# Pacing three background tasks of a decoder block: the last gate, the second lot's operands and the final residual

## The chip, the cores and the metric

One core of one Trainium2 chip. The metric is the device time of one execution in microseconds, as the median of several runs.

## The reference

One decoder layer over 512 tokens of width 2048, in float32. A token mixer comes first (two attentions, gates, an output projection). Then the part that the change touches:

```python
x = x + (1 + gt1) * mixer(...)
h = rmsnorm(x, g_ffn) * (1 + sc2) + sh2
u = h @ w_up                                   # 2048 -> 2 * 5632
u = conv_b + sum(conv_w[i] * up[:, i:i + S] for i in range(3))   # causal, per channel
a, b = split(u, 2)
x = x + (1 + gt2) * ((silu(a) * b) @ w_down)   # 5632 -> 2048
out = rmsnorm(x, g_final)
# sh1, sc1, gt1, sh2, sc2, gt2 = split(silu(c) @ w_ada + b_ada, 6)
```

`gt2` is the "last gate": a product of the 2048 values of `silu(c)` with a 2048 x 2048 matrix.

## The kernel before

All large products run on TensorE (PE) in three passes: a weight tile is loaded (`load`, the `raw` buffers, eight of them, on the queue of SyncE, SP), rounded to a high part by ScalarE (ACT, L133, `wh`), and the rest is formed by VectorE (DVE, L135, `wl`). `mm3` (L143 to L145) then multiplies high by high, high by low and low by high. `F` is a set of 62 buffers of 128 x 512 that hold operands and results.

A tile framework orders the instructions of each engine by its own plan, from dependences, free buffers and the order in the program. Each engine then works in that order, and waits at an instruction until its data is there. `behind(pin)` adds one rule: what is written inside it stands after `pin` on `pin`'s engine.

Stages after the mixer: the output projection with the second norm at its end; a plain up-projection of the first three channel tiles (`plain`, L1095); then 41 units (`unit`, L207), each of which multiplies a pair of weight tiles with the normed tokens by Strassen-Winograd's scheme in seven products. A unit calls `between` twice, with its latest ACT and DVE instructions as pins. `finish` adds the convolution and the activation, and POOL stores the tile to `yd` in memory; the first three units also finish the three plain tiles.

The down-projection takes the 44 channel tiles in five lots: six plain, sixteen by Strassen (`strassen_down`, once for each half of the columns, with four groups and a call of `step` after each group of its two passes), two plain, sixteen by Strassen, and four plain. Partial sums go to memory (`sumd`) by accumulating DMAs of POOL (`add_to`). Each Strassen lot needs operand forms (`pair_forms`): sums, differences and splits of the tiles in `yd`, made before their group.

Three tasks run beside this:
- `last_gate` (L1167): 32 times, load half a row block of the gate's matrix into `soft` (one buffer), scale it by `silu(c)` on ACT, and accumulate it in memory; then sum over the partitions in four steps. `run(gate)` advances it by one step ahead of each unit.
- `forms2` (L1226): the forms of the second Strassen lot, whose tiles are loaded into the same `soft`.
- the end: for each of four token blocks and four column blocks, the last plain lot's four tiles are multiplied, `sumd` is added, the gate applied, and the residual `x1t` accumulated by a POOL DMA (in the last block it is loaded and added by DVE); squares are summed on ACT, and each token block is scaled and stored.

Of the kernel before, what the change touches and what calls it, by code (L numbers as in the profile page):

```python
# [36 lines left out]
NU = 3  # L37
# [39 lines left out]
def block_kernel(ctx: ExitStack, tc: tile.TileContext, A: dict, out: bass.AP):  # L77
# [7 lines left out]
    def nm(s):  # L85
        counter[0] += 1
        return f"{s}_{counter[0]}"
# [4 lines left out]
    def slot(dt=F32):  # L92

        return t2k("F", SLOTS, dt)
# [29 lines left out]
    def load(src, w=1024):  # L124
        raw = t2k("raw", 8, w=w)
        pins["load"] = nc.sync.dma_start(raw, src)
        return raw
# [2 lines left out]

    def parts(raw, w=1024):
        wh = t2k("wh", 3, F32R, w)
        act(wh, raw, AF.Copy)  # L133
        wl = t2k("wl", 3, F32R, w)
        tt(wl, raw, wh.bitcast(F32), ALU.subtract)  # L135
        return wh, wl

    def prep(src, w=1024):
# [21 lines left out]
    def split(src, hi=None, lo=None):  # L160
        hi = slot(F32R) if hi is None else hi
        pins["hi"] = act(hi, src, AF.Copy)
        lo = slot(F32R) if lo is None else lo
        tt(lo, src, hi.bitcast(F32), ALU.subtract)  # L164
        return hi, lo
# [6 lines left out]
    def form_t(f, b1, b2):  # L172

        t = t2k("sp", 2)
        tt(t[:, :HALF], b1[:, HALF:], b1[:, :HALF], ALU.subtract)
        tt(t[:, HALF:], b2[:, HALF:], t[:, :HALF], ALU.subtract)
        f["T1"], f["T2"] = halves(split(t))

    def form_u(f, b1, b2):
        t = t2k("sp", 2)  # L180
        tt(t[:, :HALF], b2[:, HALF:], b1[:, HALF:], ALU.subtract)
        tt(t[:, HALF:], b2[:, :HALF], b1[:, :HALF], ALU.subtract)
        tt(t[:, HALF:], t[:, HALF:], t[:, :HALF], ALU.subtract)
        f["T3"], f["T4"] = halves(split(t))
# [3 lines left out]
    def room(p):  # L188

        if p % 2 == 0:  # L190
            shared["B11"] = slot(F32R), slot(F32R)
        return tuple(x[:, p % 2 * HALF : (p % 2 + 1) * HALF] for x in shared["B11"])
# [549 lines left out]
    def run(work, n=1):  # L742
        for _ in range(n):
            last = next(work, None)
        return last
# [232 lines left out]
    def turn():  # L978

        if to_turn:  # L980
            j, x = to_turn.pop(0)
            ps = outs()
            for b in range(NQB):
                nc.tensor.transpose(ps[:, b * P : (b + 1) * P], x[:, b * P : (b + 1) * P], ident)
            o = slot()
            act(o, ps, AF.Copy)
            save(x1t[:, :, j * P : (j + 1) * P], o.rearrange("p (b f) -> p b f", b=NQB))
# [96 lines left out]
    def finish(j, ua, ub):  # L1084
        a = conv(ua, 2 * j)
        act(a, a, AF.Silu)
        b = conv(ub, 2 * j + 1)
        tt(a, a, b, ALU.mult)
        nc.gpsimd.dma_start(yd[j // 2][:, j % 2 * S : (j % 2 + 1) * S], a)
# [75 lines left out]
    gate_sum = [dr.tile([P, 1024], F32, tag=f"gates{half}", name=f"gates{half}") for half in range(2)]  # L1165

    def last_gate():  # L1167
        for k in range(KT):
            for half in range(2):
                w = sb.tile([P, 1024], F32, tag="soft", name=nm("soft"))  # L1170
                save(w, A["w_gate"][k, :, half * 1024 : (half + 1) * 1024])
                yield
                act(w, w, AF.Copy, scale=c_col[:, k : k + 1])  # L1173
                save(gate_sum[half], w, **({"accum_op": ALU.add} if k else {}))
        for b in range(4):
            w = sb.tile([P, 1024], F32, tag="soft", name=nm("soft"))
            save(w[:, :S], gate_sum[b // 2][:, b % 2 * S : (b % 2 + 1) * S])
            save(w[:1, S:], A["b_gate"][:, b * S : (b + 1) * S])
            yield
            ps = outs()  # L1180
            mm(ps[:1], ones[:, :1], w[:, :S], start=True, stop=True)
            stt(w[:1, S:], ps[:1], 1.0, w[:1, S:], ALU.add, ALU.add)
            save(gate_row[:, b * S : (b + 1) * S], w[:1, S:])

    gate = last_gate()
    for j in range(NU, NJ):
        run(gate)
        if j < 2 * NU:
            finish(j - NU, *ups[2 * (j - NU) : 2 * (j - NU) + 2])
        elif j < 2 * NU + 2:  # L1190
            x = t2k("T", 2)
            save(x, x1d[KT - 2 + j - 2 * NU])
            to_turn.append((KT - 2 + j - 2 * NU, x))
        finish(j, *unit(A["w_up"][j - NU], f, lambda *_: turn()))

# [12 lines left out]
    def plain_down(src, y, pairs, done):  # L1210

        n = 2 * len(pairs)
        for b in range(4):
            ps = bank(b)
            for c, p in enumerate(pairs):
                w = prep(src[b, c])
                if b == 0:
                    y.extend(two_tiles(p))
                for i in range(2):
                    k = 2 * c + i  # L1220
                    for t in range(NQB):
                        mm3(ps[t], cols(y[k], t), cols(w, i, S), k == 0, k == n - 1)
            for t in range(NQB):
                done((t, b), evac(ps[t]))

    def pair_forms(f, first, own=False):  # L1226
        for p in range(MID // 2):
            if own:
                r = sb.tile([P, 1024], F32, tag="soft", name=nm("soft"))
                nc.sync.dma_start(r, yd[first // 2 + p])  # L1230
            else:
                r = load(yd[first // 2 + p])
            b1, b2 = r[:, :S], r[:, S:]
            f[p]["B11"] = split(b1[:, :HALF], *room(p))
            form_t(f[p], b1, b2)
            form_u(f[p], b1, b2)
            f[p]["B21"], f[p]["B22"] = halves(split(b2))
            yield

    def strassen_down(v, src, f, done, step=lambda i: None):  # L1240
# [59 lines left out]
        add_to(sumd[tb], c)  # L1300

    f1, f2 = ([{} for _ in range(MID // 2)] for _ in range(2))
    forms1, forms2 = pair_forms(f1, AT[1]), pair_forms(f2, AT[3], True)
    made = [0]

    def first_sum(tb, c):
# [5 lines left out]
    plain_down(A["w_down0"], [], range(D0 // 2), first_sum)  # L1312
    run(forms1, MID)
    strassen_down(0, A["w_down1"][0], f1, keep)
    strassen_down(1, A["w_down1"][1], f1, keep, lambda i: run(forms2) if i in (2, 4, 6) else None)

    def second_sum(tb, c):
        keep(tb, c)
        if tb[0] == NQB - 1:
            run(forms2)  # L1320

    plain_down(A["w_down2"], [], range(AT[2] // 2, AT[3] // 2), second_sum)
    run(forms2, MID)


    base = {}

    def sum_here(tb, c):
        add_to(c, sumd[tb])
        base[tb] = c  # L1330

    strassen_down(0, A["w_down3"][0], f2, keep)
    y, last_w = [], {}

    def last_operands(i):
        if i == 3:
            for p in range(AT[4] // 2, NJ // 2):
                y.extend(two_tiles(p))
        elif i > 3:
            last_weights(i - 4)  # L1340
# [6 lines left out]

    strassen_down(1, A["w_down3"][1], f2, sum_here, last_operands)


    def row_of(src, b):
        r = slot()
        save(r, src[:, b * S : (b + 1) * S].to_broadcast([P, S]))
        return r

    row, g_row = ([row_of(src, b) for b in range(4)] for src in (gate_row, A["g_row"]))
    ps = []
    for t in range(NQB):
        xs = []
        s = sb.tile([P, NQB], F32, tag="s", bufs=2, name=nm("s"))  # L1360
        r = sb.tile([P, NQB], F32, tag="r", bufs=2, name=nm("r"))
        for b in range(2):
            base[t, b] = fetch(sumd[t, b])
        late = t == NQB - 1
        if late:
            before = [fetch(x1t[:, t, b * S : (b + 1) * S]) for b in range(4)]
        for b in range(4):
            if not ps:
                ps = bank(t)
            o = ps.pop(0)  # L1370
            for k in range(D2):
                mm3(o, cols(y[k], t), last_w[b, k], k == 0, k == D2 - 1)
            x = base[t, b]
            tt(x, o, x, ALU.add)
            tt(x, x, row[b], ALU.mult)
            if late:
                tt(x, x, before[b], ALU.add)
            else:
                add_to(x, x1t[:, t, b * S : (b + 1) * S])
            act(t2k("ta", 2), x, AF.Square, accum_out=s[:, b : b + 1])  # L1380
            if late and b < 2:
                tt(x, x, g_row[b], ALU.mult)
            xs.append(x)
        tt(r[:, :2], s[:, :2], s[:, 2:], ALU.add)
        tt(r[:, 2:3], r[:, :1], r[:, 1:2], ALU.add)
        act(r[:, 3:], r[:, 2:3], AF.Sqrt, scale=1.0 / D, bias=eps)
        nc.vector.reciprocal(r[:, 3:], r[:, 3:])
        for b, x in enumerate(xs):
            if late and b < 2:
                act(x, x, AF.Copy, scale=r[:, 3:])  # L1390
            else:
                stt(x, x, r[:, 3:], g_row[b], ALU.mult, ALU.mult)
            nc.sync.dma_start(out[t][:, b * S : (b + 1) * S], x)


def _layout(i):
# [101 lines left out]
```

## Time and profile before

| | us |
|---|---|
| median of 3 runs | 2950.79 (2948.07 to 2954.95) |
| the profiled execution | 2941.89 |
| its span, first to last instruction | 2940.1 |
| PE busy | 2804.4 (95%) |
| DVE busy | 2421.0 (82%) |
| ACT busy | 1465.1 (50%) |

Times in the profile count from the span's start. Lines such as L1173 are lines of the kernel before. In a group's line the last numbers are the idle time of the engine just before these instructions and what ended it; in a timeline that stands in brackets. An instruction's time includes its own latency, so that of two in a row on one engine the second can start before the first has ended.

### The profile page before, as it was taken

What the parts mean: (1) busy time and instruction counts of PE and PEld (TensorE: products, weight loads), DVE (VectorE), ACT (ScalarE), POOL (GpSimd) and SP (SyncE); (2) the same over time, 40 slices, a digit from 0 to 9 for tenths busy, and PEclk for the clock granted to TensorE, in tenths of its full rate; (3) what the DMA queues carried; (4) which work ended last, traced back from release to release, by engine and by line L of the source; (5) the groups of instructions that cost most, each with busy time, mean ns of one, the idle gap of its engine ahead of it and who ended that gap; (6) DMA issues with size and microseconds to landing.
All of it is one profiled execution on the core that took longest, in us unless ns stands there. A gap on an engine that the chain in (4) does not pass through costs nothing.

```text
span 2940.1 us, 47740 instructions
## 1 busy us (share of the span) xinstructions
PE 2804.4 (95%) x18780; PEld 2567.8 (87%) x18780; DVE 2421.0 (82%) x3452; ACT 1465.1 (50%) x2066; POOL 331.3 (11%) x549
## 2 busy tenths in 40 slices
PE   9999999999999999999988878999999999998996
PEld 7779999999997778899878878999999998886785
DVE  8979889888887998798666667889888897887784
ACT  5554444555547555344565444545545445545452
POOL 0000000100111211112311111000000000002103
PEclk9999999999999999999998889999999999999998
DMA  9954456555574658667766666333333336568657
GB/s 357 334 203 159 152 193 209 194 178 170 184 235 147 233 203 283 226 182 224 238 160 172 179 172 167 116 127 109 119 128 110 130 116 208 157 170 224 174 179 191
DMA packets 161637, 544.84 MB, mean 185 GB/s; under 512 B 21170, under 2 KB 21554, under 8 KB 161412
## 3 DMA queue, kind: packets, MB, share of 16 engines
q1 hardware_dynamic: 109156, 384.88, 39.6%
q0 software_dynamic: 51664, 156.52, 19.1%
q8 instruction: 147, 2.41, 0.3%
q14 instruction: 78, 0.64, 0.1%
q10 hardware_dynamic: 592, 0.39, 0.0%
HBM read 450.57 MB, written 87.73 MB: 183 GB/s over the span
## 4 chain that ended last, share of the span: by engine, by line
PE 70%; DMA 10%; issue 8%; DVE 8%; ACT 2%; POOL 2%; SPq 0%; POOLq 0%; DVEq 0%; ACTq 0%
PE att L145 11%; PE att L143 11%; PE att L144 11%; PE acc L143 11%; PE acc L145 11%; PE acc L144 11%; DMA gates<-soft 2%; DMA soft<-in_w_gate 2%; DVE wl L135 2%; DVE raw L290 2%; DVE F L164 1%; DMA raw<-in_w_va 1%; DMA soft<-yd 1%; DMA F<-x1t 1%; PE acc L709 1%
## 5 line engine op out<-in xcount | busy, mean ns | idle before, releaser
L133 ACT ACTIVATE wh<-raw 128x1024 fp32r<-128x1024 f32 (+2 forms) x795 | 832.2, 1051 | 992.1 <-PE acc L144 181.0
L135 DVE TENSOR_TENSOR wl<-raw,wh 128x1024 fp32r<-128x1024 f32 (+2 forms) x795 | 958.9, 1210 | 209.6 <-ACT wh L133 202.8
L143 PE MATMUL acc<-F,wh 128*128 128x256 f32 (+1 forms) x2504 | 733.2, 295 | 28.0 <-ACT wh L133 14.1
L145 PE MATMUL acc<-F,wl 128*128 128x256 f32 (+1 forms) x2504 | 735.9, 294 | 5.3 <-DVE wl L135 5.2
L143 PE MATMUL att<-F,wh 128*128 128x256 f32 (+1 forms) x2432 | 716.1, 297 | 23.5 <-ACT wh L133 19.3
L144 PE MATMUL acc<-F,wh 128*128 128x256 f32 (+1 forms) x2504 | 735.8, 294 | 0.0
L145 PE MATMUL att<-F,wl 128*128 128x256 f32 (+1 forms) x2432 | 718.4, 296 | 9.8 <-DVE wl L135 9.8
L144 PE MATMUL att<-F,wh 128*128 128x256 f32 (+1 forms) x2432 | 717.7, 295 | 1.2 <-DVE F L164 1.2
L143 PEld LDWEIGHTS acc<-F,wh 128*128 128x128 f32 x2504 | 483.5, 193 | 43.5 <-ACT wh L133 17.0
L143 PEld LDWEIGHTS att<-F,wh 128*128 128x128 f32 x2432 | 474.5, 195 | 37.3 <-ACT wh L133 22.0
L145 PEld LDWEIGHTS acc<-F,wl 128*128 128x128 f32 x2504 | 483.5, 193 | 16.4 <-DVE wl L135 7.5
L144 PEld LDWEIGHTS acc<-F,wh 128*128 128x128 f32 x2504 | 484.0, 193 | 9.9 <-DVE F L164 0.8
L145 PEld LDWEIGHTS att<-F,wl 128*128 128x128 f32 x2432 | 473.6, 195 | 20.5 <-DVE wl L135 13.1
L144 PEld LDWEIGHTS att<-F,wh 128*128 128x128 f32 x2432 | 474.6, 195 | 11.8 <-DVE F L164 4.3
L290 DVE SCALAR_TENSOR_TENSOR raw<-raw,raw 128x1024 f32<-128x1024 f32 x154 | 186.2, 1217 | 9.1 <-ACT raw L323 7.8
L143 PE MATMUL att<-wh,F 128*128 128x512 f32 x448 | 178.7, 400 | 10.4 <-ACT F L414 7.1
L144 PE MATMUL att<-wl,F 128*128 128x512 f32 x448 | 176.2, 393 | 5.0 <-DVE wl L135 5.0
L145 PE MATMUL att<-wh,F 128*128 128x512 f32 x448 | 175.6, 392 | 1.0 <-DVE F L164 1.0
L233 DVE TENSOR_TENSOR raw<-raw,raw 128x1024 f32<-128x1024 f32 x81 | 98.5, 1216 | 19.4 <-DMA raw<-in_w_x 14.8
L1173 ACT ACTIVATE soft<-soft,c_col 128x1024 f32<-128x1024 f32 x32 | 36.8, 1150 | 155.3 <-DMA soft<-in_w_gate 155.3
L144 PE MATMUL acc<-wl,F 128*128 128x512 f32 x288 | 112.4, 390 | 0.4 <-DVE wl L135 0.4
L145 PE MATMUL acc<-wh,F 128*128 128x512 f32 x288 | 112.2, 390 | 0.0
(350 smaller groups left out, 3730.2 us busy)
## 6 DMA issues: line engine op xcount, KB each, us to landing
raw<-in_w_up SPq DMA_DIRECT2D x164, 512.0 KB, 3.6
raw<-in_w_ada SPq DMA_DIRECT2D x154, 512.0 KB, 5.5
raw<-in_w_x SPq DMA_DIRECT2D x128, 512.0 KB, 4.3
raw<-in_w_down SPq DMA_DIRECT2D x104, 512.0 KB, 4.3
xd<-F POOLq DMA_DIRECT2D x64, 256.0 KB, 3.0
F<-xd POOLq DMA_DIRECT2D x64, 256.0 KB, 5.0
raw<-in_w_o SPq DMA_DIRECT2D x32, 512.0 KB, 4.5
soft<-in_w_gate POOLq DMA_DIRECT2D x32, 512.0 KB, 4.6
```

The source lines that it names most:

```text
L133: act(wh, raw, AF.Copy)
L135: tt(wl, raw, wh.bitcast(F32), ALU.subtract)
L143: mm(ps, ah, bh, start=first, stop=False, skip_group_check=not check)
L144: mm(ps, ah, bl, start=False, stop=False, skip_group_check=not check)
L145: return mm(ps, al, bh, start=False, stop=last, skip_group_check=not check)
L164: tt(lo, src, hi.bitcast(F32), ALU.subtract)
L233: last_v = tt(s, a21, a22, ALU.add)
L290: stt(raw, raw, 1.0, cb[half], ALU.mult, ALU.mult, accum_out=macc[:, t, half : half + 1])
L709: mm(dots[:, :W], both[:, b * P : (b + 1) * P], kiR[i][:, :W], start=i == 0, stop=i == 1)
L1173: act(w, w, AF.Copy, scale=c_col[:, k : k + 1])
```

## The change

Three things. The gate's loads go to SP; a step now ends after the load and again after the accumulate, and is called inside each unit, behind its pins. The second lot's tiles go by turns into `soft` and into the two `ta` buffers, each loaded one step before its use; their forms stand behind the splits of the group before. For the first two column blocks, gate and residual are applied to the partial sums beside the last Strassen half (`base_steps`) and written back; in the end only the last product times the gate is added there, and for the other two column blocks the residual is loaded a token block ahead. A token block's scaling and stores stand behind the second column block of the next.

```diff
     def parts(raw, w=1024):
-        act(wh, raw, AF.Copy)
+        pins["wh"] = act(wh, raw, AF.Copy)
-        tt(wl, raw, wh.bitcast(F32), ALU.subtract)
+        pins["wl"] = tt(wl, raw, wh.bitcast(F32), ALU.subtract)
...
     def last_gate():
         for k in range(KT):
             for half in range(2):
-                save(w, A["w_gate"][k, :, half * 1024 : (half + 1) * 1024])
+                nc.sync.dma_start(w, A["w_gate"][k, :, half * 1024 : (half + 1) * 1024])
                 yield
                 act(w, w, AF.Copy, scale=c_col[:, k : k + 1])
                 save(gate_sum[half], w, **({"accum_op": ALU.add} if k else {}))
+                yield
         for b in range(4):
             # both loads: save -> nc.sync.dma_start
...
             save(gate_row[:, b * S : (b + 1) * S], w[:1, S:])
+            yield
+
+    def beside_up(i, *pins):
+        turn()
+        with behind(*pins):
+            run(gate)
...
     for j in range(NU, NJ):
-        run(gate)
...
-        finish(j, *unit(A["w_up"][j - NU], f, lambda *_: turn()))
+        finish(j, *unit(A["w_up"][j - NU], f, beside_up))
...
-                if b == 0:
+                if len(y) < 2 * c + 2:
                     y.extend(two_tiles(p))
...
+    def pair_ahead(first, p):
+        src = yd[first // 2 + p]
+        if p % 2:
+            r = t2k("ta", 2), t2k("ta", 2)
+        else:
+            both = sb.tile([P, 1024], F32, tag="soft", name=nm("soft"))
+            r = both[:, :S], both[:, S:]
+        for i in range(2):
+            nc.sync.dma_start(r[i], src[:, i * S : (i + 1) * S])
+        return r
+
+    def forms_ahead(f, first):
+        n = MID // 2
+        r = [pair_ahead(first, p) for p in range(2)]
+        yield
+        for p in range(n):
+            if 1 <= p < n - 1:
+                r.append(pair_ahead(first, p + 1))
+            with behind(pins["wh"], pins["wl"]):
+                make_forms(f[p], p, *r[p])      # the body of pair_forms
+            yield
...
-    strassen_down(1, A["w_down1"][1], f1, keep, lambda i: run(forms2) if i in (2, 4, 6) else None)
+    y = []
+    def second_forms(i):
+        if i in (0, 1, 3, 5, 7):
+            run(forms2)
+        if i == 6:
+            y.extend(two_tiles(AT[2] // 2))
+    strassen_down(1, A["w_down1"][1], f1, keep, second_forms)
...
-        if tb[0] == NQB - 1:
+        if tb in ((NQB - 1, 1), (NQB - 1, 3)):
             run(forms2)
...
-    run(forms2, MID)
-    strassen_down(0, A["w_down3"][0], f2, keep)
+    strassen_down(0, A["w_down3"][0], f2, keep, lambda i: run(forms2) if i < 2 else None)
+    row0 = []                                   # two columns blocks of gate_row, in "ta"
+    def base_steps():
+        for n in range(10):
+            if n >= 2:
+                tb, x = at_work[n - 2]
+                save(sumd[tb], x)
+            if 1 <= n < 9:
+                (t, b), x = at_work[n - 1]
+                with behind(pins["wl"]):
+                    tt(x, x, row0[b], ALU.mult)
+                add_to(x, x1t[:, t, b * S : (b + 1) * S])
+            if n < 8:
+                tb = n % NQB, n // NQB
+                at_work.append((tb, fetch(sumd[tb])))
+            yield
...
     def last_operands(i):
+        run(bases)
...
-    row, g_row = ([row_of(src, b) for b in range(4)] for src in (gate_row, A["g_row"]))
+    row, g_row = rows_of(gate_row), rows_of(A["g_row"])   # two 128 x 1024 "raw" buffers each, over SP
...
+    x1_part = operands(0)                       # fetch sumd[t, 0:2] and x1t of column blocks 2 and 3
     for t in range(NQB):
+        ahead = operands(t + 1) if t + 1 < NQB else None
...
             x = base[t, b]
-            tt(x, o, x, ALU.add)
-            tt(x, x, row[b], ALU.mult)
-            # add_to(x, x1t[...]), or tt(x, x, before[b], ALU.add) in the last token block
-            act(t2k("ta", 2), x, AF.Square, accum_out=s[:, b : b + 1])
+            if b < 2:
+                part = t2k("w", 2)
+                tt(part, o, row[b], ALU.mult)
+                tt(x, x, part, ALU.add)
+            else:
+                tt(x, o, x, ALU.add)
+                tt(x, x, row[b], ALU.mult)
+                last = tt(x, x, x1_part[b - 2], ALU.add)
+            act(t2k("sp", 2), x, AF.Square, accum_out=s[:, b : b + 1])
...
+            if b == 1 and before:
+                finish_tokens(*before)          # reciprocal root, scaling and stores, as before
+        before = t, xs, s
+        x1_part = ahead
+    finish_tokens(*before)
```

More of the change, by code (lines that the diff above doesn't have):

```diff
@@ L1174, in last_gate @@
                 save(gate_sum[half], w, **({"accum_op": ALU.add} if k else {}))
+                yield
         for b in range(4):
             w = sb.tile([P, 1024], F32, tag="soft", name=nm("soft"))
-            save(w[:, :S], gate_sum[b // 2][:, b % 2 * S : (b % 2 + 1) * S])
-            save(w[:1, S:], A["b_gate"][:, b * S : (b + 1) * S])
+            nc.sync.dma_start(w[:, :S], gate_sum[b // 2][:, b % 2 * S : (b % 2 + 1) * S])
+            nc.sync.dma_start(w[:1, S:], A["b_gate"][:, b * S : (b + 1) * S])
             yield
@@ L1224, in plain_down, with pair_forms, make_forms @@
                 done((t, b), evac(ps[t]))
-    def pair_forms(f, first, own=False):
+    def pair_forms(f, first):
         for p in range(MID // 2):
[L1228 to L1237, printed above, removed]
+            r = load(yd[first // 2 + p])
+            make_forms(f[p], p, r[:, :S], r[:, S:])
+            yield
+    def make_forms(q, p, b1, b2):
+        q["B11"] = split(b1[:, :HALF], *room(p))
+        form_t(q, b1, b2)
+        form_u(q, b1, b2)
+        q["B21"], q["B22"] = halves(split(b2))
+    def pair_ahead(first, p):
[17 more added lines that the diff above has]
+                make_forms(f[p], p, *r[p])
             yield
@@ L1302, in block_kernel @@
     f1, f2 = ([{} for _ in range(MID // 2)] for _ in range(2))
-    forms1, forms2 = pair_forms(f1, AT[1]), pair_forms(f2, AT[3], True)
+    forms1, forms2 = pair_forms(f1, AT[1]), forms_ahead(f2, AT[3])
     made = [0]
@@ L1314, in block_kernel @@
     strassen_down(0, A["w_down1"][0], f1, keep)
-    strassen_down(1, A["w_down1"][1], f1, keep, lambda i: run(forms2) if i in (2, 4, 6) else None)
+    y = []
[5 more added lines that the diff above has]
+    strassen_down(1, A["w_down1"][1], f1, keep, second_forms)
     def second_sum(tb, c):
         keep(tb, c)
-        if tb[0] == NQB - 1:
+        if tb in ((NQB - 1, 1), (NQB - 1, 3)):
             run(forms2)
-    plain_down(A["w_down2"], [], range(AT[2] // 2, AT[3] // 2), second_sum)
-    run(forms2, MID)
+    plain_down(A["w_down2"], y, range(AT[2] // 2, AT[3] // 2), second_sum)
     base = {}
+    strassen_down(0, A["w_down3"][0], f2, keep, lambda i: run(forms2) if i < 2 else None)
+    y, last_w = [], {}
+    row0 = []
+    for b in range(2):
+        row0.append(t2k("ta", 2))
+        save(row0[b], gate_row[:, b * S : (b + 1) * S].to_broadcast([P, S]))
+    at_work = []
+    def base_steps():
[12 more added lines that the diff above has]
+            yield
     def sum_here(tb, c):
@@ L1330, in sum_here @@
         base[tb] = c
-    strassen_down(0, A["w_down3"][0], f2, keep)
-    y, last_w = [], {}
+    bases = base_steps()
     def last_operands(i):
+        run(bases)
         if i == 3:
@@ L1348, in block_kernel, with rows_of, operands, finish_tokens @@
     strassen_down(1, A["w_down3"][1], f2, sum_here, last_operands)
[L1351 to L1354, printed above, removed]
-    row, g_row = ([row_of(src, b) for b in range(4)] for src in (gate_row, A["g_row"]))
-    ps = []
+    run(bases, 10)
+    def rows_of(src):
+        both = [t2k("raw", 8, w=1024) for _ in range(2)]
+        for v, r in enumerate(both):
+            nc.sync.dma_start(r, src[:, v * 1024 : (v + 1) * 1024].to_broadcast([P, 1024]))
+        return [both[b // 2][:, b % 2 * S : (b % 2 + 1) * S] for b in range(4)]
+    row, g_row = rows_of(gate_row), rows_of(A["g_row"])
+    def operands(t):
+        for b in range(2):
+            base[t, b] = fetch(sumd[t, b])
+        return [fetch(x1t[:, t, b * S : (b + 1) * S]) for b in range(2, 4)]
+    def finish_tokens(t, xs, s):
+        r = sb.tile([P, NQB], F32, tag="r", bufs=2, name=nm("r"))
+        tt(r[:, :2], s[:, :2], s[:, 2:], ALU.add)
+        tt(r[:, 2:3], r[:, :1], r[:, 1:2], ALU.add)
+        act(r[:, 3:], r[:, 2:3], AF.Sqrt, scale=1.0 / D, bias=eps)
+        nc.vector.reciprocal(r[:, 3:], r[:, 3:])
+        for b, x in enumerate(xs):
+            if t == NQB - 1 and b < 2:
+                act(x, x, AF.Copy, scale=r[:, 3:])
+            else:
+                stt(x, x, r[:, 3:], g_row[b], ALU.mult, ALU.mult)
+            nc.sync.dma_start(out[t][:, b * S : (b + 1) * S], x)
+    ps, before = [], None
+    x1_part = operands(0)
     for t in range(NQB):
+        ahead = operands(t + 1) if t + 1 < NQB else None
         xs = []
         s = sb.tile([P, NQB], F32, tag="s", bufs=2, name=nm("s"))
[L1361 to L1366, printed above, removed]
         for b in range(4):
@@ L1373, in block_kernel @@
             x = base[t, b]
-            tt(x, o, x, ALU.add)
-            tt(x, x, row[b], ALU.mult)
-            if late:
-                tt(x, x, before[b], ALU.add)
-            else:
-                add_to(x, x1t[:, t, b * S : (b + 1) * S])
-            act(t2k("ta", 2), x, AF.Square, accum_out=s[:, b : b + 1])
-            if late and b < 2:
+            if b < 2:
+                part = t2k("w", 2)
+                tt(part, o, row[b], ALU.mult)
+                tt(x, x, part, ALU.add)
+            else:
+                tt(x, o, x, ALU.add)
+                tt(x, x, row[b], ALU.mult)
+                last = tt(x, x, x1_part[b - 2], ALU.add)
+            act(t2k("sp", 2), x, AF.Square, accum_out=s[:, b : b + 1])
+            if t == NQB - 1 and b < 2:
                 tt(x, x, g_row[b], ALU.mult)
             xs.append(x)
[L1384 to L1393, printed above, removed]
+            if b == 1 and before:
[3 more added lines that the diff above has]
+    finish_tokens(*before)
 def _layout(i):
```

## The prediction

> **What bounds the kernel now.** First the page: the share and clock of the engines in 40 slices, and the costliest groups.
>
> ```profile
> span 2940.1 us, 47740 instructions
> ...
> PE   9999999999999999999988878999999999998996
> ...
> PEclk9999999999999999999998889999999999999998
> ...
> L1173 ACT ACTIVATE soft<-soft,c_col 128x1024 f32<-128x1024 f32 x32 | 36.8, 1150 | 155.3 <-DMA soft<-in_w_gate 155.3
> ...
> raw<-in_w_up SPq DMA_DIRECT2D x164, 512.0 KB, 3.6
> ```
>
> TensorE is busy nearly throughout; what is to be won are its holes. They lie in three places: slices 20 to 24, slices 36 and 37, and the last. One ScalarE group sat idle 155.3 us, always for the same load. The busy times by stretch give the sizes (the second number is the length, then PE, PEld, DVE, ACT, POOL with counts, clock, DMA share, GB/s):
>
> ```profile
> 1424.00:1448.00 24.00, 19.68 (x139) 19.17 (x137) 10.59 (x17) 10.15 (x16) 9.83 (x18) 0.86 0.87 282
> 1448.00:1540.00 92.00, 76.04 (x461) 66.81 (x461) 61.07 (x127) 55.10 (x94) 13.69 (x22) 0.95 0.64 184
> 1540.00:1830.00 290.00, 241.33 (x1731) 233.45 (x1732) 191.66 (x227) 135.84 (x174) 42.40 (x63) 0.89 0.65 173
> 1830.00:2276.00 446.00, 446.00 (x3719) 446.00 (x3719) 397.17 (x466) 222.67 (x289) 11.91 (x22) 1.00 0.36 119
> 2596.00:2672.00 76.00, 76.00 (x337) 62.86 (x336) 61.05 (x71) 37.83 (x46) 5.74 (x7) 1.00 0.64 185
> 2672.00:2705.00 33.00, 23.08 (x101) 18.16 (x99) 22.05 (x34) 14.97 (x25) 10.47 (x12) 0.95 0.88 208
> 2705.00:2791.00 86.00, 79.55 (x335) 63.66 (x336) 66.59 (x80) 42.15 (x53) 11.29 (x13) 0.98 0.66 175
> 2791.00:2868.00 77.00, 76.58 (x338) 63.07 (x337) 63.28 (x69) 40.93 (x52) 7.56 (x10) 1.00 0.60 178
> 2868.00:2912.00 44.00, 43.97 (x194) 36.06 (x193) 23.23 (x41) 8.12 (x21) 20.62 (x31) 1.00 0.90 217
> 2912.00:2940.00 28.00, 0.00 (x0) 0.00 (x0) 13.17 (x26) 6.92 (x20) 2.87 (x4) 0.59 0.51 154
> ```
>
> From 1830 on, PE runs without a hole: 446.00 / 3719 = 0.1199 us a matmul of 256 columns, so 20.15 us a unit (7 products of 8 x 3). The 512-column ones take 76.00 / 337 = 0.2255 us. The same units before 1830 cost much more.
>
> **Why they do.** The gate's chain, from the timeline (POOL, then ACT):
>
> ```profile
> 1564.89 0.87 POOL L1174 DMA_DIRECT2D gates<-soft  x1 [7.82 <-ACT soft L1173]
> 1570.47 0.55 POOL L1171 DMA_DIRECT2D soft<-in_w_gate  x1 [4.72 <-DMA gates<-soft]
> 1575.89 0.86 POOL L1174 DMA_DIRECT2D gates<-soft  x1 [4.87 <-ACT soft L1173]
> 1434.03 1.15 ACT L1173 ACTIVATE soft<-soft,c_col 128x1024 f32<-128x1024 f32 x1 [6.09 <-DMA soft<-in_w_gate]
> 1455.88 1.15 ACT L1173 ACTIVATE soft<-soft,c_col 128x1024 f32<-128x1024 f32 x1 [1.79 <-DMA soft<-in_w_gate]
> 1537.28 1.15 ACT L1173 ACTIVATE soft<-soft,c_col 128x1024 f32<-128x1024 f32 x1 [4.75 <-DMA soft<-in_w_gate]
> 1574.44 1.15 ACT L1173 ACTIVATE soft<-soft,c_col 128x1024 f32<-128x1024 f32 x1 [6.41 <-DMA soft<-in_w_gate]
> ```
>
> One buffer: load, scale, accumulate to memory, load again, 11 us a round (1564.89 to 1575.89). Nothing paces it: it runs from before 1434 on as fast as it can, and each scaling stands at the head of ScalarE's queue while its data is under way. Behind it wait the splits that feed PE.
>
> **Term 1, the units (1540 to 1830).** At 0.1199 us the 1731 matmuls need 207.6 of 290 us; 82.4 are lost, 48.7 idle and the rest to the clock (0.89). With a pin behind the unit's own evacuation, and two turns a unit of load / scale and add, one gate step spreads over 20 us, the round of 11 us fits, and the load is issued nearly a unit before the scaling that needs it. What is late next: VectorE. It works 397.17 / 446 x 20.15 = 17.9 us a unit, and the first three units carry a second finish:
>
> ```profile
> L1080 DVE SCALAR_TENSOR_TENSOR w<-F,cw,w 128x511 f32<-128x511 f32 x44 | 32.7, 744 | 0.0
> L1088 DVE TENSOR_TENSOR w<-w,w 128x512 f32<-128x512 f32 x23 | 15.7, 682 | 0.0
> ```
>
> 4 x 0.744 + 0.682 = 3.7 us, so 21.6 against 20.15: 4.4 us over three units, and 3 for the start. Gain 75 (38, if the 32 scalings of 1.15 us came onto the path, to 82). The four summing steps keep their matmuls: no change. POOL sheds 32 issues of 0.55 us and never again waits for an accumulate to land; nobody waits for that.
>
> **Term 2, the plain up stage (1448 to 1540).** 9 tiles go in two halves (9 x 36 x 0.1199 = 38.8), 7 whole (7 x 18 x 0.2255 = 28.4): 67.2 of 92 us, 24.8 lost. Eight gate steps waited here (first and last quoted), all now behind unit 0. DVE (61.07) and ACT (55.10 less 8 x 1.15) stay under 67.2. The norm's second half, the last forms and the evacuation before unit 0 keep 9. Gain 16 (8 to 24.8).
>
> **Term 3, the end of the output projection.** The first step waited 6.09 us ahead of the norm's last pieces. Lost in 24 us: 4.3 idle and 0.14 x 24 = 3.4 of clock. The norm's chain has waits of its own: 4 (0 to 7.7).
>
> **Term 4, the second lot's forms.** The chain that ended last, then ACT's timeline:
>
> ```profile
> 2690.00 9.57 DMA soft<-yd
> ```
>
> ```profile
> 2699.59 0.42 ACT L162 ACTIVATE F<-soft 128x256 fp32r<-128x256 f32 x1 [11.04 <-DMA soft<-yd]
> ```
>
> Again one buffer, with ACT standing for the load; the evacuations behind it hold PSUM, and PE stands. From 2672 to 2791, 96 + 336 matmuls need 97.4 of 119 us: 21.6 lost. With two buffers each load is out a step (10 us or more) ahead of its use, over the 9.57 of the worst. The eight loads become sixteen of half the size; SP issues one in 0.33 us (row below) and idles otherwise: nothing. The price moves to 2596:2672, where up to two more pairs go (nine DVE operations each, of 512 columns or fewer, so at most the 0.68 us of such a row in term 6) and the two splits of the plain pair, now read ahead: 61 + 20 x 0.68 = 74.7 of 76 us, close under. I charge 2 there (0 to 5), and 5 for handovers that stay. Gain 14 (5 to 21).
>
> **Term 5, base steps beside the last unit pair (2791 to 2868).** Eight multiplies of 0.68 us make DVE 68.7 of 77. Eight fetches, accumulates and saves of 256 KB are 6.3 MB, 82 GB/s on top of 178; the stretches at 208 and 217 have a DMA share near 0.9, and the chain already passes through a weight load here:
>
> ```profile
> 2838.34 5.37 DMA raw<-in_w_down
> ```
>
> That load took 5.37 where 3.6 is usual for its size. Cost 3: three weight loads late by some 1 to 2 us each; 0 if the tiles are far enough ahead, 6 if a multiply also waits for its fetch with the splits behind it on DVE, or the steps' three buffers out of the 62 `F` are short. On POOL a save waits for its accumulate's landing, with only the next steps behind it. The wide rows now come over SP behind the last weights, in four issues where POOL had eight: nothing, while they land before the first block's sums.
>
> **Term 6, the tail.** PE's last matmul, ACT's wait, the last evacuation, the last stores:
>
> ```profile
> 2911.58 0.39 PE L145 MATMUL outs<-F,F 128*128 128x512 f32 x1
> 2919.94 0.63 ACT L1380 ACTIVATE ta<-F 128x512 f32<-128x512 f32 x1 [6.59 <-DMA F<-x1t]
> 2928.61 0.68 DVE L1374 TENSOR_TENSOR F<-outs,F 128x512 f32<-128x512 f32 x1
> 2934.38 1.95 SPq L1393 DMA_DIRECT2D out_x<-F  x4
> ```
>
> The span ends 28.1 us after PE, because the residual comes by accumulates that stand in a row. With it fetched ahead, DVE has ten operations a token block, and four more for the block before, whose end now stands behind the second column block: 14 x 0.68 = 9.5 of PE's 48 x 0.2255 = 10.8 us, so it keeps up. In this execution it took 2940.1 - 2928.6 = 11.5 us from the last evacuation to the end, with the same work in it; plus 1 of backlog, 12.5. Gain 15.6 (17 without backlog, 9 with a whole block's ending and evacuations, 14 x 0.68 less 2, in the way). The squares move to another buffer: nothing.
>
> **Sum.** 75 + 16 + 4 + 14 - 3 + 15.6 = 121.6 against the profiled execution's 2941.89: 2820.3. The median of the runs, 2950.79, is 8.9 higher; I forecast 2829 for it.
>
> **Rivals.**
> Down-projection gives it back: DVE at 74.7 of 76 and DMA near 0.9 cost what terms 4 and 6 bring; 2829 + 30 = 2859. For it: those shares. Against: the stretch from 1830 holds PE full with DVE at 89%.
>
> The scalings stay on the path, 32 x 1.15 = 37: 2866. For it: every wide split passes ACT. Against: ACT is at half (222.67 of 446).
>
> The change doesn't do all that it says, because the lost clock isn't from the holes: 0.11 x 290 = 32 stays, 2861. Two stretches:
>
> ```profile
> 1616.00:1618.00 2.00, 0.66 (x4) 0.48 (x4) 2.00 (x4) 1.95 (x3) 0.89 (x2) 1.00 0.79 260
> 1620.00:1623.00 3.00, 3.00 (x16) 3.00 (x16) 1.44 (x2) 1.05 (x1) 0.00 (x0) 0.50 0.87 311
> ```
>
> A hole under 2 us, then half clock; and none from 1830 to 2276, where there are no holes. So the clock follows even short holes, and comes back with them. [...]
>
> Slower: SP blocks the weights. The gate's loads now wait on SP for the accumulate before, and the up-projection's loads stand behind them.
>
> ```profile
> 1879.69 0.33 SPq L126 DMA_DIRECT2D raw<-in_w_up  x1
> 1896.02 1.21 DVE L233 TENSOR_TENSOR raw<-raw,raw 128x1024 f32<-128x1024 f32 x1
> 1898.47 0.37 ACT L269 ACTIVATE F<-att 128x256 f32<-128x256 f32 x1
> ```
>
> A tile loaded at 1879.69 (3.6 to land) is used at 1896.02: 12.7 us of lead. The scaling follows 1898.47, its accumulate lands some 7 us on (round above), at 1906; the next such loads are due 1896 to 1900. If the gate's load stood ahead of them they would come 10 us late, still inside the lead. Were the accumulate itself late, behind a store on POOL, the lead would be used up: from 16.3 us on, each of 36 units loses 3.6 and the kernel ends at 2829 + 130 = 2959. Against: in planned order the accumulate follows the scaling, so those loads should come first. [...]
>
> **Numbers.** Forecast 0.66 (own range 2808 to 2848), down-projection 0.13, scalings 0.10, clock 0.04, SP 0.03, others 0.04. The range 2804 to 2868 takes in the first four. Faster by over 0.2% (about what a measurement here can tell) 0.95, the same 0.02, slower 0.03.
>
> **What would show it.** Right: the scaling's idle (155.3) gone, PE full from unit 3 on at clock 1.0, its loads 20 us apart to about 2200; no ACT wait for yd; 12 to 13 us after the last matmul. Wrong: ACT or SP waits on soft in the units, PE holes before 2672 of today's scale, multiplies waiting for fetches in the last pair, rows late in the tail.

## The result

| | before | after |
|---|---|---|
| median of the runs, us | 2949.57 (4 runs, 2948.07 to 2954.95) | 2815.76 (4 runs, 2810.95 to 2819.28) |
| ratio after / before | | 0.9542 [0.9523, 0.9561] |
| profiled execution, us | 2941.89 | 2819.28 |
| PE / DVE / ACT busy | 95% / 82% / 50% | 98% / 86% / 52% |

The kernel became 134 us faster; the forecast was 2829, a gain of 122. Lines are those of the kernel after (the gate's load is L1172, its scaling L1174, its accumulate L1175), and in an experiment's fences those of its own kernel. First the page of the kernel after: PE and its clock in 40 slices, and the gate's loads.

```profile
span 2817.4 us, 47873 instructions
...
PE   9999999999999999999999999999999999999997
...
PEclk9999999999999999999999999999999999999998
...
soft<-in_w_gate SPq DMA_DIRECT2D x32, 512.0 KB, 3.8
```

Every slice but the last is full, at full clock: the two dents in the middle are gone, and the one at the end is smaller. The groups by line show the cause of the largest one gone as well, for the scaling that had 155.3 us of idle time before it:

```profile
L1174 ACT ACTIVATE soft<-soft,c_col 128x1024 f32<-128x1024 f32 x32 | 36.6, 1142 | 0.0
```

Busy times by stretch of the kernel after (columns as in the prediction): end of the output projection, plain up stage, first four units, the other units, last Strassen half, the last plain lot, the rest.

```profile
1433.00:1452.00 19.00, 17.17 (x141) 16.74 (x140) 11.40 (x20) 9.89 (x16) 8.85 (x16) 1.00 1.00 338
1452.00:1522.00 70.00, 69.24 (x460) 63.79 (x460) 62.24 (x128) 49.58 (x88) 2.67 (x5) 1.00 0.39 128
1526.00:1607.00 81.00, 80.23 (x664) 79.49 (x663) 74.05 (x91) 48.13 (x64) 7.59 (x12) 1.00 0.57 171
1607.00:2170.00 563.00, 563.00 (x4694) 563.00 (x4694) 500.67 (x587) 310.88 (x393) 40.40 (x57) 1.00 0.64 171
2674.00:2753.00 79.00, 77.31 (x337) 62.52 (x336) 65.76 (x73) 41.13 (x52) 16.93 (x24) 1.00 0.87 257
2753.00:2797.00 44.00, 44.00 (x196) 36.45 (x195) 29.03 (x51) 9.56 (x25) 17.17 (x27) 1.00 0.73 214
2797.00:2817.00 20.00, 0.52 (x3) 0.09 (x1) 12.46 (x25) 5.42 (x14) 0.00 (x0) 0.63 0.29 105
```

From 1607 on, behind the first four, the units run at 563.00 / 4694 = 0.1199 us a matmul. Two rows are worse than they need be: the last Strassen half takes 79 us where before's took 77, and 20 us follow the last matmul. Cut at the first and last matmul of each part, and set against the profiled execution of before, the terms came out so:

| term | forecast | measured | lengths, before and after |
|---|---|---|---|
| 1 units | -75 | -80.9 | 915.0, 834.1 |
| 2 plain up stage | -16 | -21.1 | 91.4, 70.3 |
| 3 end of the output projection | -4 | -5.8 | 30.0, 24.2 |
| 4 second lot's forms, down-projection up to the last half | -14 | -18.0 | 336.5, 318.5 |
| 5 last Strassen half | +3 | +2.3 | 76.9, 79.2 |
| 6 tail, last plain lot to the end | -15.6 | -8.2 | 71.8, 63.6 |
| sum | -121.6 | -131.7 | |

The first 1420 us, which the change does not touch, were 9.1 us longer in this execution of after than in that of before, so the two spans differ by 122.7 only. Over the 13 profiled executions of all kernels here the first matmul of the plain up stage came between 1446 and 1455 us, so that part varies by as much.

### The profile page after: what moved, and what is told of

It reads as the page before. It is cut to its first block, busy times and chain, and to the rows that moved or that the text cites. A ratio compares the mean times of both kernels' runs of the same rounds, so it can differ in the third digit from the quotient of the medians.

```text
span 2817.4 us, 47873 instructions
## 1 busy us (share of the span) xinstructions
PE 2763.3 (98%) x18780; PEld 2535.6 (90%) x18780; DVE 2427.0 (86%) x3464; ACT 1467.8 (52%) x2066; POOL 314.8 (11%) x519
## 4 chain that ended last, share of the span: by engine, by line
PE 73%; DVE 6%; DMA 4%; issue 3%; ACT 1%; POOL 0%; DVEq 0%; POOLq 0%; ACTq 0%; SPq 0%
PE att L145 12%; PE att L143 12%; PE att L144 12%; PE acc L145 10%; PE acc L143 10%; PE acc L144 10%; DVE wl L135 1%; DMA raw<-in_w_x 1%; PE acc L709 1%; PE acc L803 1%; PE outs L909 1%; DMA F<-sumd 1%; DMA F<-x1d 1%; PE acc L878 1%; DMA raw<-in_w_down 1%
## 5 line engine op out<-in xcount | busy, mean ns | idle before, releaser
L145 PE MATMUL att<-F,wl 128*128 128x256 f32 (+1 forms) x2432 | 710.2, 292 | 2.9 <-DVE wl L135 2.9
L144 PE MATMUL att<-F,wh 128*128 128x256 f32 (+1 forms) x2432 | 710.1, 292 | 1.2 <-DVE F L164 1.2
L143 PE MATMUL att<-F,wh 128*128 128x256 f32 (+1 forms) x2432 | 706.9, 293 | 2.9 <-DVE sp L273 1.6
L143 PEld LDWEIGHTS att<-F,wh 128*128 128x128 f32 x2432 | 466.3, 192 | 14.8 <-ACT wh L133 3.7
L144 PEld LDWEIGHTS att<-F,wh 128*128 128x128 f32 x2432 | 466.4, 192 | 11.9 <-DVE F L164 4.3
L145 PEld LDWEIGHTS att<-F,wl 128*128 128x128 f32 x2432 | 465.9, 192 | 12.0 <-DVE wl L135 4.6
L233 DVE TENSOR_TENSOR raw<-raw,raw 128x1024 f32<-128x1024 f32 x81 | 98.9, 1221 | 28.2 <-DMA raw<-in_w_x 21.1
L145 PE MATMUL acc<-wh,F 128*128 128x512 f32 x288 | 112.2, 389 | 0.0
L143 PE MATMUL acc<-wh,F 128*128 128x512 f32 x288 | 111.8, 390 | 0.0
```

Of the source, the lines that this page charges most:

```text
L143: mm(ps, ah, bh, start=first, stop=False, skip_group_check=not check)
L144: mm(ps, ah, bl, start=False, stop=False, skip_group_check=not check)
L145: return mm(ps, al, bh, start=False, stop=last, skip_group_check=not check)
L233: last_v = tt(s, a21, a22, ALU.add)
```

## The experiments

Theory: the gate's pace was the cost (a load-dependent scaling at the head of ACT's queue, unpaced), and POOL's queue is why the tail fell short. Each part was first run alone.

**The gate's part alone.** The kernel before with the new `last_gate`; forms and tail as before.

```diff
+    def beside_up(i, *pins):
+        turn()
+        with behind(*pins):
+            run(gate)
...
-        run(gate)
...
-        finish(j, *unit(A["w_up"][j - NU], f, lambda *_: turn()))
+        finish(j, *unit(A["w_up"][j - NU], f, beside_up))
```

> The kernel before with the gate's part of the change alone (loads on SP, two turns a step, called inside the units behind their pins). If the gate's scalings at the head of ScalarE's queue were the loss in all three stretches, this takes 5.8 + 21.1 + 80.9 = 108 us off, so about 2842 us, PE is full from the fourth unit on, and the clock stays at 1.0 there. If the other two parts of the change helped those stretches too, by freeing buffers or queues, it comes out above 2860.

2837.75 us, ratio 0.9615 [0.9596, 0.9634]: 115 of the 134 us. Its plain up stage is 70.3 us and its units 834.1, the same as in the kernel after to 0.1 us, and its down-projection keeps the holes of before. One stretch of its units, as long as the one of before that had PE at 241.33 and the clock at 0.89:

```profile
1520.00:1810.00 290.00, 289.24 (x2406) 288.50 (x2405) 260.58 (x309) 164.37 (x211) 23.09 (x34) 1.00 0.62 171
```

**Is it the queue or the pace?** Two kernels from this one. The first takes the pins away and keeps SP and the two turns a unit:

```diff
     def beside_up(i, *pins):
         turn()
-        with behind(*pins):
-            run(gate)
+        run(gate)
```

> As e1, but the steps are not held behind the unit's evacuation and sum: only the queue of the loads and their place in the program differ from before. Theory pace: nothing holds the chain back, so it again runs a round of some 10 us as fast as it can from the output projection's end on, ScalarE waits at the scaling in every round, and at least two thirds of the 108 us are lost again: 2910 to 2945 us. Rival queue: what cost the time was the load's place on POOL behind the accumulate; then this equals e1 within 6 us.

2915.97 us, ratio 0.988 [0.9861, 0.9899]. One of ACT's waits (us in total, times, longest), and the two stretches of the prediction, in the kernel without pins:

```profile
ACT soft L1174 <- DMA soft<-in_w_gate: 123.3, 30, 7.4
1448.00:1540.00 92.00, 79.62 (x488) 71.27 (x489) 66.67 (x133) 60.10 (x101) 10.82 (x16) 0.93 0.72 196
1540.00:1830.00 290.00, 254.02 (x1944) 246.69 (x1944) 211.15 (x250) 143.91 (x185) 29.76 (x40) 0.95 0.69 183
```

The scaling waits for its load 30 times again, and holes and clock loss are back. Without the pins the plan puts the steps ahead of their units: the loads are issued from 1430.75 on in rounds of 9 to 19 us instead of once a unit. Of the part's 115 us the pins carry 78 (2915.97 less 2837.75). The other 37 are the rest of the edit: two turns a step, the call inside the unit, and SP.

The second keeps the pins and puts the loads back on POOL (those of the summing steps too):

```diff
-                nc.sync.dma_start(w, A["w_gate"][k, :, half * 1024 : (half + 1) * 1024])
+                save(w, A["w_gate"][k, :, half * 1024 : (half + 1) * 1024])
```

> As e1, but the gate's loads stay on POOL's queue; the pins stay. Theory pace: a round of 11 us fits into a unit of 20 us on either queue, so this equals e1 within 6 us (0.2%). Rival queue: POOL stands for each accumulate to land, the loads come late and each of 32 steps costs 1 to 4 us: 2875 to 2950 us.

2837.08 us, ratio 0.9611 [0.9596, 0.9626]: the same as on SP. Its units are 834.1 us too. So with the pins the queue of these loads is worth nothing; what counts is where the step stands in the engines' order and how often it is called. How the 37 us divide was not tried: no kernel has the pins with one turn a unit.

**The second lot's forms alone.** The kernel before with `forms_ahead`, the two buffers and the steps behind each group.

```diff
-    forms1, forms2 = pair_forms(f1, AT[1]), pair_forms(f2, AT[3], True)
+    forms1, forms2 = pair_forms(f1, AT[1]), forms_ahead(f2, AT[3])
...
-    strassen_down(1, A["w_down1"][1], f1, keep, lambda i: run(forms2) if i in (2, 4, 6) else None)
+    strassen_down(1, A["w_down1"][1], f1, keep, second_forms)
...
-    strassen_down(0, A["w_down3"][0], f2, keep)
+    strassen_down(0, A["w_down3"][0], f2, keep, lambda i: run(forms2) if i < 2 else None)
```

> The kernel before with the second lot's part alone (two buffers by turns, loads a step ahead, forms behind the splits, plain tiles read ahead). If ScalarE standing for the tiles of the second lot was the loss between the second Strassen half and the last one, 17 to 18 us go: about 2932 us, with PE holes from 2672 to 2742 closed and at most 2 us of new ones before. If the weights or the accumulating DMAs were late by themselves, the holes stay and it is 2950 us within 6.

2937.96 us, ratio 0.9951 [0.9933, 0.9968]. From the second half of the first lot to the end of the first half of the second it takes 77.6 + 22.0 + 77.6 us, where before took 78.2 + 30.4 + 86.4: 17.8 less, and 14.6 by the medians. ACT's waits for these tiles from the middle of that stretch on, in the kernel before and then in this one:

```profile
ACT F L162 <- DMA soft<-yd: 23.2, 7, 11.0
```

```profile
ACT F L162 <- DMA soft<-yd: 2.0, 1, 2.0
```

Seven waits have become one.

**The end alone.** The kernel before with `base_steps` and the new tail.

```diff
     def last_operands(i):
+        run(bases)
...
-    row, g_row = ([row_of(src, b) for b in range(4)] for src in (gate_row, A["g_row"]))
+    row, g_row = rows_of(gate_row), rows_of(A["g_row"])
...
+    x1_part = operands(0)
     for t in range(NQB):
+        ahead = operands(t + 1) if t + 1 < NQB else None
```

> The kernel before with the end's part alone (base steps beside the last Strassen half, residual a block ahead, a block's ending one block later). By the two traces it should bring 8.2 us in the tail and cost 2.3 in the last Strassen half: 6 us net, 0.2%. By the forecast's term 6 it would bring 12 to 13 us net. The trace should show VectorE waiting some 8 us for the first fetch of a partial sum in the tail, as in the changed kernel.

2943.68 us, ratio 0.9972 [0.996, 0.9985], some 8 us less. The time after the last matmul is 17.6 us, not 12.5, and the last Strassen half 79.0. So the shortfall against the forecast's tail comes with this part alone, if smaller than in the kernel after. By the medians the three parts, each alone, bring 114.8, 14.6 and 8.3 us, 137.7 in sum, against 133.8 together.

**Why the tail is long.** In the kernel after, DVE's timeline at the start of the tail and at its end:

```profile
2757.70 0.68 DVE L1455 TENSOR_TENSOR w<-att,raw 128x512 f32<-128x512 f32 x1
2759.47 0.69 DVE L1455 TENSOR_TENSOR w<-att,raw 128x512 f32<-128x512 f32 x1 [1.09 <-PE att L145]
2762.19 0.69 DVE L1458 TENSOR_TENSOR F<-att,F 128x512 f32<-128x512 f32 x1 [2.03 <-PE att L145]
2770.73 0.69 DVE L1456 TENSOR_TENSOR F<-F,w 128x512 f32<-128x512 f32 x1 [7.84 <-DMA F<-sumd]
...
2806.05 0.68 DVE L1458 TENSOR_TENSOR F<-outs,F 128x512 f32<-128x512 f32 x1
```

L1455 multiplies a product by the gate, L1456 adds it to the partial sum, which comes 7.84 us after DVE is ready for it; L1458 adds a product of the other column blocks to its partial sum. POOL's timeline tells why:

```profile
2744.90 0.90 POOL L647 DMA_DIRECT2D F<-sumd  x1
2753.09 0.55 POOL L1377 DMA_DIRECT2D sumd<-F  x1 [7.28 <-DMA F<-x1t]
...
2755.64 5.52 POOL L1207 DMA_DIRECT2D F<-sumd  x6
2758.87 3.42 POOL L1377 DMA_DIRECT2D sumd<-F  x2
2763.76 1.07 POOL L647 DMA_DIRECT2D F<-sumd  x2 [1.48 <-DMA F<-sumd]
```

The first fetches of the tail (L647, 2763.76; the L647 of 2744.90 is still a base step's) stand in one queue behind a write-back that waits 7.28 us for the accumulate before it, behind the accumulates of the last half's sums, and behind two more write-backs. The theory is this queue. Rivals: the write-back and second fetch alone make the sums late; or buffers come late whatever the queue. First the write-backs were taken away: the bases stay in their `F` buffers.

```diff
-            if n >= 2:
-                tb, x = at_work[n - 2]
-                save(sumd[tb], x)
...
+                base[t, b] = x
...
-        for b in range(2):
-            base[t, b] = fetch(sumd[t, b])
```

> The changed kernel, but the eight gated sums of the base steps stay in their F buffers: not written back to memory, and not fetched again for the tail. Theory: the tail is 20 us and not 12.5 after the last matmul because VectorE waits 7.8 us for the first of these fetches, which stands on POOL behind the accumulates of the last Strassen half, and 9.5 of 10.8 us of work a block leaves no room to catch up. Then 7 to 8 us go (ratio to the changed kernel 0.9973, about 2808), with 12 to 13 us from the last matmul to the end. Rival: the residual's fetches or the accumulates behind them are as late; then 2 us or less go.

2810.18 us, ratio 0.9522 [0.9508, 0.9536]; 16.1 us after the last matmul, better than 20.0 and short of the forecast's 12.5. The write-backs were part of it only: the wait moved to the residual, whose fetch has the same place on POOL:

```profile
2766.98 0.69 DVE L1456 TENSOR_TENSOR F<-F,F 128x512 f32<-128x512 f32 x1 [5.37 <-DMA F<-x1t]
```

Then the base steps were left out, and all four column blocks got gate and residual in the tail, fetched a token block ahead:

```diff
     def last_operands(i):
-        run(bases)
...
-            if b < 2:
-                part = t2k("w", 2)
-                tt(part, o, row[b], ALU.mult)
-                tt(x, x, part, ALU.add)
...
+            tt(x, o, x, ALU.add)
+            tt(x, x, row[b], ALU.mult)
+            last = tt(x, x, x1_part[b], ALU.add)
```

> The changed kernel without the base steps: gate and residual of all four column blocks are applied in the tail, with sums and residual fetched a block ahead. VectorE then has 16 x 0.68 = 10.9 us a block against PE's 10.8. The last Strassen half should lose its 2.3 us of holes. If writing back and fetching again is what delays the tail, the fetches come early here, and the tail ends 14 to 18 us after PE (now 20): 4 to 8 us faster than the changed kernel. If the base steps are worth what they take off VectorE, the tail ends 22 us or more after PE, and it is no faster.

2807.94 us, ratio 0.9513 [0.95, 0.9527]. The last half is back at 76.6 us, and 15.0 follow the last matmul, again with a wait for a fetch on POOL:

```profile
2752.34 0.69 DVE L1446 TENSOR_TENSOR F<-att,F 128x512 f32<-128x512 f32 x1 [5.36 <-DMA F<-sumd]
```

The base steps spare DVE operations in the tail; without them the tail is no longer, and the last half gets 2.6 us back.

**The queue by itself.** In each of the three kernels the tail's fetches went to SP (`fetch_sp` is a fetch issued there), with the kernel after run beside them. The edit to the kernel after; those to the other two are alike:

```diff
     def operands(t):
         for b in range(2):
-            base[t, b] = fetch(sumd[t, b])
-        return [fetch(x1t[:, t, b * S : (b + 1) * S]) for b in range(2, 4)]
+            base[t, b] = fetch_sp(sumd[t, b])
+        return [fetch_sp(x1t[:, t, b * S : (b + 1) * S]) for b in range(2, 4)]
```

> The kernel after, with the tail's fetches (the partial sums of the first two column blocks and the residual of the other two) issued on SP instead of POOL; nothing else differs. Theory (POOL's in-order queue: the fetches stand behind the six accumulates that end the last Strassen half, each waiting for an evacuation): VectorE's waits of 1.78 and 7.84 us for the first partial sums go, the stretch after the last matmul falls from 20.0 to 13 to 15 us, the time by 4 to 7 us against the kernel after. Rival (the fetches are late because their buffers come free late or because the write-backs land late, on whatever queue): the waits stay, under 1.5 us gained.

> The kernel without base steps (all four column blocks get gate and residual in the tail), with the tail's fetches on SP. Theory (POOL's queue): the waits of 5.36 and 1.78 us for the first partial sum go, 15.0 after the last matmul becomes 12 to 13, about 10 us faster than the kernel after. Rival (VectorE is short of room in the tail itself, 4 x 3 + 2 operations and the ending of the block before for each of four blocks): 15 stays, as without SP, about 8 us faster than the kernel after.

> The kernel with the bases of the first two column blocks kept in their buffers, with the residual of the other two fetched on SP. Theory (POOL's queue): the wait of 5.37 us for the residual goes, 16.1 after the last matmul becomes 12 to 13, about 7 us faster than the kernel after. Rival (buffers of F late): 16 stays.

> The kernel after itself, unchanged, timed beside the three others on one chip, so that they can be compared with it directly: 2812 to 2820, 20 us after the last matmul.

| | median, us | ratio to before | last Strassen half | after the last matmul |
|---|---|---|---|---|
| after, again | 2816.54 (2812.23 to 2818.08) | 0.954 [0.9525, 0.9555] | 78.7 | 19.0 |
| after, fetches on SP | 2807.26 (2804.59 to 2809.74) | 0.9512 [0.9497, 0.9527] | 79.0 | 12.0 |
| bases kept, on SP | 2806.81 (2806.31 to 2809.15) | 0.9512 [0.9498, 0.9527] | 78.4 | 12.9 |
| no base steps, on SP | 2804.30 (2800.89 to 2805.40) | 0.95 [0.9486, 0.9515] | 76.9 | 12.6 |

One changed queue takes 9 us off the kernel after by the medians, a little more than the 4 to 7 expected. Of the 10.7 us between the two profiled executions 7.0 lie after the last matmul, where 12.0 are left; the rest lies ahead of the tail, 2.4 of it before the plain up stage, and is not shown to be the queue's. In the other two kernels the same move shortens that stretch by 3.2 us (16.1 to 12.9) and 2.4 (15.0 to 12.6). From the timelines of SP and DVE, and the last stretch, of that kernel:

```profile
2744.00 1.50 SPq L1424 DMA_DIRECT2D F<-sumd  x2
2752.82 0.68 DVE L1460 TENSOR_TENSOR w<-att,raw 128x512 f32<-128x512 f32 x1
2753.54 0.69 DVE L1461 TENSOR_TENSOR F<-F,w 128x512 f32<-128x512 f32 x1
2794.35 0.68 DVE L1463 TENSOR_TENSOR F<-outs,F 128x512 f32<-128x512 f32 x1
2793.00:2805.00 12.00, 0.46 (x3) 0.04 (x1) 5.78 (x12) 3.07 (x7) 0.00 (x0) 0.73 0.38 131
```

SP issues the first fetches at 2744.00, six microseconds before the last half ends (in the kernel after, POOL did so ten microseconds behind that end). The add (L1461) follows its product (L1460) at once: no wait of DVE for a fetch is longer than 1.0 us. SP too waits for write-backs to land there, 17.6 us in three waits, so it is not their landing by itself that held DVE. And the tail follows DVE's first wait for a sum: 5.8 us with the end alone, 6.9 in the second run of the kernel after and 7.84 in the first go with 17.6, 19.0 and 20.0 us after the last matmul.

In the tail the queue of the plain fetches counts, by 7.0 us, because on POOL they stood behind accumulates and write-backs of other blocks. The gate's loads stand behind an accumulate too, but one whose landing they need on either queue, since both use the one buffer: POOL waits for it 216.0 us in 31 waits, SP 229.5 in 30, and moving them was worth nothing. The rival that DVE lacks room in the tail is out for the kernel without base steps too: 12.6 against 15.0. That kernel is the fastest by the medians: it beats the kernel after by 12 us, without overlap of the runs. So the base steps, one of the three parts of the change, bring nothing once the fetches are early (2807.26 with them, 2804.30 without).

## Why the prediction was right, and where it was off

Terms 1 to 3 were right in mechanism. The signs asked for are there: the scaling's idle is gone, PE is full from the units' start but for 0.8 us, and from the second on the loads come 17 to 25 us apart. They were undersized by 5.9, 5.1 and 1.8 us, mostly since the deductions did not come in full: by their first matmuls the first five units took 20.59, 20.82, 21.47, 20.44 and 20.48 us, 3.0 us above 20.15 in sum where 7.4 was charged, and the plain stage keeps 3 of the 9 us of evacuation and last forms charged there. The loss itself was a little larger than read: of the 1731 matmuls 12 are small ones that turn tiles, and the first ten units of before, taken one by one, lost 84.0 us and not 82.4. The splits of the 41 units hide the scalings wholly: that rival (2866) is refuted by the 0.0 of idle time and by units at PE's own pace.

Term 4 was undersized by 4.0. The crowded half came as charged, or nearly: from its own first to its last matmul the second half of the first lot, where the work went, takes 77.8 us where it took 76.4, 1.4 of the 2 charged, and the hole behind it is gone (77.6 against 78.2 to the next part's first matmul). Of the 5 us for handovers 1.9 stayed: 22.0 + 77.3 against the 97.4 that the matmuls need. Down-projection as a place that gives the gain back is refuted, except for these 1.4 us and its last half.

Term 5 was right: +2.3 where +3 was forecast, and +1.5 to +2.1 in the other kernels with base steps. Late weight loads are there as it said: in the last half ACT waits four times for one ahead of a rounding, 5.2 us in sum, in the kernel without base steps, with the fetches on SP, once, 1.6. Without base steps the 2.3 are gone. The 5.37 us that it took for a slow load, against 3.6, is no outlier, though: the median of these loads in this half of before is 5.1. The kernel with the gate's loads on POOL, which has no base steps either, has 78.6 us there, so a part of this size can also come otherwise.

Term 6 is the step that failed: forecast 12.5 us after the last matmul, 20.0 measured. Of its two pieces one held. From the last evacuation to the end of the span it is 2817.4 - 2806.05 = 11.4 us, forecast 11.5. The other, the backlog, was put at 1 us and was 2806.05 - 2797.4 = 8.6. The prediction said of the residual "with it fetched ahead", and never put these fetches in POOL's order behind the accumulates of the last half and the write-backs of its own base steps. Of a base step's save it said that it waits "with only the next steps behind it"; the tail's fetches stood behind it as well. DVE, with 9.5 of 10.8 us a token block, could catch up only part of a late start: its first sum started 16.9 us after the tail's first matmul, against 3.8 with the fetches on SP. On SP the pieces are 2805.5 - 2794.35 = 11.2 and 0.9 us, which is the forecast's tail.

**The 8.9 us for the median.** This step was wrong too. The excess of the median over the profiled execution was carried over to the kernel after as if it lay in parts that stay. Two kernels that leave the units as they were, the one with the forms alone and the one with the end alone, show the same 290 us:

```profile
1540.00:1830.00 290.00, 234.56 (x1655) 226.35 (x1655) 183.31 (x218) 130.47 (x166) 42.41 (x63) 0.88 0.65 169
1547.00:1837.00 290.00, 237.58 (x1686) 229.47 (x1686) 185.82 (x220) 131.91 (x168) 42.45 (x63) 0.88 0.66 172
```

Against 1731 matmuls in the execution of before that is 76 and 45 fewer, at 0.1199 us 9.1 and 5.4 us. Their first part was 0.5 shorter and 6.6 us longer than in it. So the execution that the sum was made against lost less in the holes than these two, and the change takes the holes away whatever they cost. Two executions are few: this is the likely reading, not more. 2820.3 without the 8.9, less the 10.1 by which the terms were undersized in sum, is 2810; the unchanged first part varies by as much as what is left to 2815.76. That the forecast was only 13 us off is in part luck: terms 1 to 5 brought 17.5 us more than forecast and term 6 brought 7.4 less. With the tail as forecast, in the kernel with the fetches on SP, the median is 2807.26, at the low edge of the own range of 2808 to 2848.

**The lost clock.** The rival that it does not come from the holes is refuted: the clock is 1.00 in each kernel whose holes are closed (1520 to 1810 above) and 0.95 in the one without pins, whose holes are closed in part. By holes: in the 290 us of before (clock 0.89) PE had 35 of over 0.05 us with 48.7 us in sum, the longest 5.32, 5.28 and 4.51 us; without pins (0.95) 35 with 36.0 us. Short ones went with lost clock too: in the kernel before no hole from 1578.1 to 1620 was longer than 1.70 us, and the clock was 0.55 from 1606 to 1609.5 and 0.50 from 1620 to 1623. Which length of hole is enough was not tried.

**SP blocks the weights.** The mechanism of this rival is there, its price is not. In the units of the kernel after SP stands for the accumulate of the gate once a unit, and the weights stand behind it:

```profile
SPq L1172 <- DMA gates<-soft: 231.9, 30, 8.6
1889.82 0.33 SPq L1172 DMA_DIRECT2D soft<-in_w_gate  x1
1891.40 10.85 SPq L126 DMA_DIRECT2D raw<-in_w_up  x4
1910.46 0.33 SPq L1172 DMA_DIRECT2D soft<-in_w_gate  x1
1911.56 10.85 SPq L126 DMA_DIRECT2D raw<-in_w_up  x4
```

This is the sign that the prediction listed under "wrong" (SP waits on `soft` in the units), and the argument "in planned order those loads should come first" was false. But 231.9 / 30 = 7.7 us a unit is inside the 12.7 us of lead worked out there, no engine waits for a weight load in these units, and with the gate's loads off SP the units take the same 834.1 us.

## What to carry to other kernels

When an engine that feeds the bottleneck stands for a background task's load, look where its instruction stands in that engine's order before looking at the transfer: tying it behind the work of its unit was worth 78 us here, another queue for the same load, once it was tied, nothing. When a fetch is moved "ahead", write down the queue that issues it with everything in front of it: seven microseconds hung on plain fetches standing behind accumulates and write-backs. And an offset between a profiled execution and the median may only be carried to the new kernel if it lies in parts that stay.

## What was not expected of the hardware

Holes cost more than their own length, again in the kernel without pins: 254.02 us of PE work for 1944 matmuls, where 1944 at 0.1199 us are 233.1, so 20.9 us of 290 went on slower matmuls (clock 0.95) beside 36.0 of idle time. In the kernel before it was 33.7 (clock 0.89) beside 48.7. In the units of the kernel after, with all holes under 0.4 us, the clock is 1.00, and from 1607 on, without a hole, a matmul takes 0.1199 us.
